# A Mamba-2 mixer block on one Trainium2 core: the decay matrices of two heads in one tile, with one exponential and one product for both

## The chip, the cores and the metric

The kernel runs on one core of one Trainium2 chip. The metric is the device time of one execution in microseconds (us), as the median of several runs. The engines have the names that the profile uses: PE (TensorE, matrix products), PEld (its loading of stationary operands), DVE (VectorE), ACT (ScalarE), POOL (GpSimd) and SP (SyncE, which issues the DMAs here). Each engine takes its instructions in order from a queue of its own, and engines wait for each other on semaphores.

## What is computed

One encoder block on a sequence of 1024 positions with 1024 channels in float32: a mixer (a gated convolution branch and a Mamba-2 branch, merged) and a gated feed-forward network, each with its normalisation. The change lies in the Mamba-2 branch. It has 32 heads of 64 channels in 4 groups of 8 heads; the heads of a group share the state inputs B and C of width 128. Cut to what matters here, the reference does in every chunk

```python
acs = jnp.cumsum(ak, axis=1)                      # ak = dt * a, per head
seg = acs[:, :, None] - acs[:, None, :]
decay = jnp.exp(jnp.where(causal, seg, -jnp.inf)) # one matrix per head
cb = jnp.einsum("blgn,bsgn->blsg", ck, bk)        # one matrix per group
y_diag = jnp.einsum("blsg,blsgj,bsgjp->blgjp", cb, decay, xk)
```

and adds the part that comes from the state of the chunks before, multiplies by a gate and normalises over a group. So each head needs the matrix `decay * cb`, and this product is what the change touches.

## The kernel before

The sequence is cut in two halves of 512 positions (`hf` 0 and 1), and the channels lie on the 128 partitions, so nearly every tile is 128 x 512. Every large matrix product is made of three float32r products (high part by high part, high by low, low by high), so PE has most of the work. The program has three parts: the first input projections (to about 650 us), the stage with the Mamba-2 branch and the remaining projections (about 650 to 1200 us, after which the feed-forward part follows).

In the middle stage two streams of work are woven into each other. The main stream is a list of projection steps (`p0_..`, `p1_..`, `co..`, `s0_..`, `wo..`), each 24 matmuls of 512 columns into a PSUM tile that DVE or ACT then empties; before its matmuls a weight block is split into a high part `wh` (ACT, L163) and a low part `wl` (DVE, L164). The PSUM tiles of these steps are a ring of three, so a step can start only when the step three before it has been emptied: in the groups of the SSM's inputs that is the last of the DVE steps of a short convolution, `xo` (L1109), after three steps `p` (L1106). The second stream is `ssd` (L495 and on), a generator that is advanced a little after every second matmul row, and beside it run the convolution branch and a few smaller ones. A scheduler then puts the instructions of all streams in an order for each engine, from its own model of the times; so an instruction that gets another shape can move others around it.

`ssd` handles one group of one half: 4 chunks of 128 positions, 4 pairs of heads (`j`). For each pair a `Decay` object makes the two matrices M:

- `load` (L550): two DMAs, each a broadcast of one head's row of cumulative sums over 128 partitions, into two tiles of 512 columns (4 chunks of 128). There are four such tiles, so two pairs can be under way.
- `exp(e)` for head e (L553 to L559): four ACT steps of 128 columns (a Relu of the difference; the bias is a column that differs by chunk), then one exponential over 512 columns.
- `mul(e)` (L562): one DVE product of 512 columns with `cbm`, the masked C B matrix of the group.

The matrices are then the moving operands of 16 small matmuls `yd` (L623; two heads by four chunks, two passes each), which also frees the tiles for the pair after the next. Beside them `yo` (L608) multiplies C by the state, E (L613) scales that, and L625 to L629 put the pair's output `y` together. The squares of the four y of a group are summed into `say` (L329), PE sums that over the partitions (`scy`, or `sc` further on, L264), and DVE makes a reciprocal square root `ry` from it in small steps (L275 to L283). PE transposes that (L292), it goes through memory, and it scales the four `y` (L652), which are written to memory and come back as operands `Hh`, `Hl` of the steps `s0_..` and `s1_..` (L217, L218). Names carry half and group: `yd033` belongs to half 0, group 3, pair 3.

The calls of the three steps of a `Decay` stand at fixed places in `ssd`: in the first four chunks for the first pair of a group, and after the output of pair j for pair j + 1.

Of the kernel before, what the change touches and what calls it, by code (L numbers as in the profile page):

```python
# [6 lines left out]
F32 = mybir.dt.float32  # L7
F32R = mybir.dt.float32r
I32 = mybir.dt.int32
AF = mybir.ActivationFunctionType  # L10
ALU = mybir.AluOpType
# [3 lines left out]
P = 128  # L15
T = 512
# [3 lines left out]
J = 8  # L20
# [50 lines left out]
def build(tc, ins, outs):  # L71
# [33 lines left out]
    act = nc.scalar.activation  # L105
    vec = nc.vector
# [388 lines left out]
    def ssd(hf, g, D):  # L495
        sp = pools["b"]
# [18 lines left out]
        for c in range(NCK):  # L515
# [3 lines left out]
        cbm = sp.tile([P, T], F32, tag="cbm", name=f"cbm{hf}{g}")  # L519
        vec.tensor_tensor(out=cbm.rearrange("p (c l) -> p c l", l=P), in0=pcb.rearrange("p (c l) -> p c l", l=P),  # L520
                          in1=tri.unsqueeze(1).to_broadcast([P, NCK, P]), op=ALU.mult)
# [19 lines left out]
            S.append(sn)  # L541

        class Decay:
            def __init__(self, j):
                self.heads, self.M = [g * J + 2 * j + e for e in range(2)], []

            def load(self):
                for hd in self.heads:
                    m = sp.tile([P, T], F32, tag="M", name=f"M{hf}{hd}", bufs=4)
                    dma(out=m, in_=acs_d[hf, hd:hd + 1, :].to_broadcast([P, T]))  # L550
                    self.M.append(m)

            def exp(self, e):  # L553
                hd, m = self.heads[e], self.M[e]
                for c in range(NCK):
                    sl = slice(c * P, (c + 1) * P)
                    act(out=m[:, sl], in_=m[:, sl], func=AF.Relu, scale=-1.0,  # L557
                        bias=acs[:, c * 32 + hd:c * 32 + hd + 1])
                act(out=m, in_=m, func=AF.Exp, scale=-1.0)  # L559

            def mul(self, e):
                vec.tensor_tensor(out=self.M[e], in0=self.M[e], in1=cbm, op=ALU.mult)  # L562

        last = hf == NH - 1
        M = Decay(0)
        sn = None
        for c in range(NCK):
            px = pstile(f"xT{hf}{g}{c}")
            for j in range(4):
                nc.tensor.transpose(out=px[:, j * P:(j + 1) * P], in_=xs[j][:, c * P:(c + 1) * P], identity=ident)  # L570
            xd = sp.tile([P, T], F32, tag="xdt", name=f"xdt{hf}{g}{c}", bufs=4)
            vec.tensor_tensor(out=v3(xd), in0=v3(px), in1=heads(dt, c, g), op=ALU.mult)
            xdt.append(xd)
            if c > 0:
                next_state(c - 1, sn)
            if not (last and c == NCK - 1):
                wx = sp.tile([P, T], F32, tag="wx", name=f"wx{hf}{g}{c}", bufs=2)
                for h in range(J):
                    hs = slice(h * 64, (h + 1) * 64)
                    o = c * 32 + g * J + h  # L580
                    act(out=wx[:, hs], in_=px[:, hs], func=AF.Copy, scale=wdec[:, o:o + 1])
                wxs.append(wx)
            if c == 0:
                M.load()
            elif c == 1:
                M.exp(0)
            elif c == 2:
                M.exp(1)
            else:
                M.mul(0)  # L590
                M.mul(1)
            yield 1
            if not (last and c == NCK - 1):
                sn = new_state(c)
            yield 1
# [3 lines left out]
        for j in range(4):  # L599
            E = sp.tile([P, T], F32, tag="E", name=f"E{hf}{g}{j}", bufs=2)  # L600
            for e in range(2):
                hd = g * J + 2 * j + e
# [12 lines left out]
            if j < 3:  # L615
                M = Decay(j + 1)
# [11 lines left out]
            vec.tensor_tensor(out=pdg[:, c0:], in0=E[:, c0:], in1=pdg[:, c0:], op=ALU.add)  # L628
            vec.tensor_tensor(out=y, in0=y, in1=pdg, op=ALU.mult)  # L629
            if j < 3:  # L630
                M.exp(0)
            yield 1
            if j < 3:
                M.exp(1)
            sq.add(y)
            ys.append(y)
            yield 1
            if j < 3:
                M.mul(0)
                M.mul(1)  # L640
        D["end", g] = (sq, ys)

    def ssd_norm(hf, g, D):
# [1130 lines left out]
```

## Time and profile before

| | us |
|---|---|
| median of 3 runs | 2087.94 |
| lowest and highest run | 2082.25, 2089.29 |
| the profiled execution, its own time | 2084.13 |
| its span, first to last instruction | 2082.4 |
| mean granted TensorE clock | 0.975 |

The profile is of one execution. Busy time counts the time in which an engine runs an instruction; a mean duration is that of one instruction from start to end, and two instructions on one engine can overlap, so the distance from one start to the next is shorter than the duration. In a row of the timeline the first number is the start in us from the start of the span, the second the length of the merged piece; a bracket at the end gives the idle time of the engine before it and what ended that. In the rows of groups the numbers behind the count are the busy time in us and the mean in ns. Tile names are given there without half and group (`M`, `xo`, `yd`).

### The profile page before, as it was taken

Reading aid. Unit: us, or ns where it says so; the run is one execution under the profiler, and the core shown is the slowest. Engines: PE = TensorE matmul, PEld = TensorE weight load, DVE = VectorE, ACT = ScalarE, POOL = GpSimd, SP = SyncE. Lnnn points to the kernel's source line nnn. Section 1 sums busy time; section 2 is a strip of 40 time slices with the busy share of each in tenths; the row PEclk is TensorE's granted clock in tenths of the full one; section 3 lists DMA queues with packets and bytes.
Section 4 is the critical chain, followed back from the end, with each engine's and each line's share of the span. In section 5 each row is a group of like instructions: output and inputs, shape, how many; then the busy total and the mean of one; then the engine's idle time right before and its main releaser. Section 6 shows DMA issues by size and latency. Waiting matters only on the chain.

```text
span 2082.4 us, 26179 instructions
## 1 busy us (share of the span) xinstructions
PE 1941.3 (93%) x8802; PEld 1548.7 (74%) x8802; DVE 1574.0 (76%) x2458; ACT 1004.0 (48%) x1938; POOL 646.8 (31%) x487
## 2 busy tenths in 40 slices
PE   4899899999998899998899999998999999989997
PEld 3788688887876677776677777776888888767876
DVE  8878989878797978989797965759543443699655
ACT  4644454443444867566555733335333333444243
POOL 0008688888870000100000000005443443331400
PEclk9999999999998999999999999999999999999998
DMA  9232222323326867789898777761422222577653
GB/s 348 86 105 93 76 97 102 116 86 107 104 86 215 271 198 237 243 294 304 266 315 264 239 247 245 250 241 64 154 81 86 85 73 101 186 244 234 202 174 119
DMA packets 163958, 366.43 MB, mean 176 GB/s; under 512 B 18744, under 2 KB 19184, under 8 KB 163824
## 3 DMA queue, kind: packets, MB, share of 16 engines
q1 hardware_dynamic: 163824, 364.77, 52.6%
q8 instruction: 69, 1.13, 0.2%
q14 instruction: 65, 0.53, 0.1%
HBM read 281.57 MB, written 83.13 MB: 175 GB/s over the span
## 4 chain that ended last, share of the span: by engine, by line
PE 59%; DVE 20%; DMA 12%; issue 4%; ACT 3%; POOL 1%; SPq 0%; DVEq 0%; ACTq 0%; POOLq 0%
PE uXp L817 10%; PE uXf L817 10%; PE uZp L817 5%; PE uZf L817 5%; PE uXd L817 3%; PE uYp L817 2%; PE uYf L817 2%; DMA M<-acs_d 2%; PE s L189 2%; PE s L187 2%; PE s L188 2%; DMA E<-eac_d 2%; DMA wa_f<-in 1%; DVE gc L1128 1%; DMA wa_m<-in 1%
## 5 line engine op out<-in xcount | busy, mean ns | idle before, releaser
L163 ACT ACTIVATE wh<-w 128x1024 fp32r<-128x1024 f32 (+1 forms) x110 | 113.4, 1032 | 108.6 <-PE s L188 37.4
L164 DVE TENSOR_TENSOR wl<-w,wh 128x1024 fp32r<-128x1024 f32 (+1 forms) x110 | 130.7, 1189 | 23.3 <-ACT wh L163 15.8
L531 POOL TENSOR_TENSOR S<-S,dt_etot 128x512 f32<-128x512 f32 x16 | 20.5, 1281 | 294.7 <-ACT S L538 138.5
L557 ACT ACTIVATE M<-M,dt_acs 128x128 f32<-128x128 f32 x256 | 80.0, 394 | 59.4 <-DMA M<-acs_d 58.6
L930 POOL TENSOR_TENSOR fw<-fw,fw 128x512 f32<-128x512 f32 x37 | 59.5, 1608 | 120.2 <-DMA fw<-in 118.6
L672 DVE SCALAR_TENSOR_TENSOR pcM<-u,cw_eo,pcM 128x512 f32<-128x512 f32 x120 | 90.2, 752 | 2.5
L672 DVE SCALAR_TENSOR_TENSOR pcQ<-u,pc,pcQ 128x512 f32<-128x512 f32 x112 | 84.3, 753 | 2.7
L187 PE MATMUL s<-Hh,wh 128*128 128x512 f32 x192 | 76.4, 402 | 6.3 <-ACT Hh L217 4.0
L672 DVE SCALAR_TENSOR_TENSOR pcR<-u,pc,pcR 128x512 f32<-128x512 f32 x104 | 78.4, 754 | 2.7
L189 PE MATMUL s<-Hh,wl 128*128 128x512 f32 x192 | 76.8, 400 | 3.6 <-DVE wl L164 3.6
L187 PE MATMUL p<-Hh,wh 128*128 128x512 f32 x144 | 62.3, 453 | 18.0 <-DVE xo L1109 9.0
L188 PE MATMUL s<-Hl,wh 128*128 128x512 f32 x192 | 77.1, 402 | 0.9 <-DVE Hl L218 0.8
L845 POOL TENSOR_TENSOR b<-Hh,Hl 128x512 f32<-128x512 f32 x4 | 5.9, 1480 | 223.3 <-DVE spare L329 211.9
L817 PE MATMUL uXp<-T2h,dp 128*128 128x512 f32 x216 | 72.0, 395 | 3.0 <-ACT dp L795 3.0
L817 PE MATMUL uZp<-B22h,ep 128*128 128x512 f32 x216 | 72.4, 397 | 2.2 <-POOL ep L796 1.6
L817 PE MATMUL uYp<-Hh,bp 128*128 128x512 f32 x216 | 72.8, 399 | 1.0 <-DVE s1g L997 1.0
L817 PE MATMUL uXp<-T3h,fp 128*128 128x512 f32 x216 | 72.0, 396 | 1.2 <-ACT s L985 0.9
L817 PE MATMUL uXp<-T4h,gp 128*128 128x512 f32 x216 | 72.5, 396 | 0.4 <-DVE s5c L997 0.4
L817 PE MATMUL uZp<-T1h,cp 128*128 128x512 f32 x216 | 72.0, 395 | 0.0
L817 PE MATMUL uXp<-Hh,ap 128*128 128x512 f32 x216 | 71.0, 390 | 0.0
L188 PE MATMUL p<-Hl,wh 128*128 128x512 f32 x144 | 61.3, 427 | 5.4 <-DVE Hl L346 5.4
L817 PE MATMUL uZf<-T1h,cf 128*128 128x512 f32 x176 | 59.4, 401 | 3.5 <-DVE g L997 3.5
(565 smaller groups left out, 6412.5 us busy)
## 6 DMA issues: line engine op xcount, KB each, us to landing
fw<-in SPq DMA_DIRECT2D x134, 512.0 KB, 3.3
w<-in SPq DMA_DIRECT2D x100, 512.0 KB, 5.1
M<-acs_d SPq DMA_DIRECT2D x64, 256.0 KB, 4.9
wa_f<-in SPq DMA_DIRECT2D x48, 256.0 KB, 3.7
wa_m<-in SPq DMA_DIRECT2D x16, 512.0 KB, 9.3
xs<-xbc_d SPq DMA_DIRECT2D x32, 256.0 KB, 6.0
E<-eac_d SPq DMA_DIRECT2D x64, 128.0 KB, 6.2
y<-z_d SPq DMA_DIRECT2D x32, 256.0 KB, 5.5
```

Source lines behind the costliest of these rows:

```text
L163: act(out=hi, in_=w[:, :nk * P], func=AF.Copy)
L164: eng.tensor_tensor(out=lo, in0=w[:, :nk * P], in1=hi.bitcast(F32), op=ALU.subtract)
L187: nc.tensor.matmul(out=out, lhsT=whi[:, sl], rhs=rh, start=first and i == 0, stop=False)
L188: nc.tensor.matmul(out=out, lhsT=whi[:, sl], rhs=rl, start=False, stop=False)
L189: nc.tensor.matmul(out=out, lhsT=wlo[:, sl], rhs=rh, start=False, stop=last and i == n - 1)
L531: gp.tensor_tensor(out=v3(sn), in0=v3(S[c]), in1=heads(etot, c, g), op=ALU.mult)
L557: act(out=m[:, sl], in_=m[:, sl], func=AF.Relu, scale=-1.0, bias=acs[:, c * 32 + hd:c * 32 + hd + 1])
L672: vec.scalar_tensor_tensor(out=pt if k < n - 1 else out or pt, in0=src(k), scalar=w(k), in1=pt, op0=ALU.mult, op1=ALU.add)
L817: nc.tensor.matmul(out=out, lhsT=l[:, sl], rhs=r, start=first and k == 0 and i == 0, stop=k == 3 and i == 2, skip_group_check=True)
L845: gp.tensor_tensor(out=t, in0=H[k][0].bitcast(F32), in1=H[k][1].bitcast(F32), op=ALU.add)
L930: e[8].tensor_tensor(out=a21, in0=a11, in1=a21, op=ALU.subtract)
L1128: vec.scalar_tensor_tensor(out=t[:, d:], in0=src[:, :T - d], scalar=wc(k), in1=t[:, d:], op0=ALU.mult, op1=ALU.add)
```

## The change

The two heads of a pair get one tile `both` of 128 x 1024, two of them in turn in place of four of 512, so the memory is the same. The two DMAs and the eight Relu steps stay, each on its half of the tile. The two exponentials become one over 1024 columns, behind the Relu steps of the second head; the two products become one over 1024 columns, whose second operand `cbm` is read twice. The matmuls take the two halves as they took the two tiles.

```diff
         class Decay:
             def __init__(self, j):
-                self.heads, self.M = [g * J + 2 * j + e for e in range(2)], []
+                self.heads = [g * J + 2 * j + e for e in range(2)]
+                self.both = sp.tile([P, 2 * T], F32, tag="M", name=f"M{hf}{g}{j}", bufs=2)
+                self.M = [self.both[:, e * T:(e + 1) * T] for e in range(2)]
             def load(self):
-                for hd in self.heads:
-                    m = sp.tile([P, T], F32, tag="M", name=f"M{hf}{hd}", bufs=4)
+                for hd, m in zip(self.heads, self.M):
                     dma(out=m, in_=acs_d[hf, hd:hd + 1, :].to_broadcast([P, T]))
-                    self.M.append(m)
-            def exp(self, e):
+            def relu(self, e):
...
-                act(out=m, in_=m, func=AF.Exp, scale=-1.0)
-            def mul(self, e):
-                vec.tensor_tensor(out=self.M[e], in0=self.M[e], in1=cbm, op=ALU.mult)
+                if e:
+                    act(out=self.both, in_=self.both, func=AF.Exp, scale=-1.0)
+            def mul(self):
+                m3 = self.both.rearrange("p (e t) -> p e t", t=T)
+                vec.tensor_tensor(out=m3, in0=m3, in1=cbm.unsqueeze(1).to_broadcast([P, 2, T]), op=ALU.mult)
...
-                M.exp(0)
+                M.relu(0)
...
-                M.exp(1)
+                M.relu(1)
...
-                M.mul(0)
-                M.mul(1)
+                M.mul()
```

The scheduler orders the middle stage anew: outside it the order of the two programs is the same on PE, DVE and ACT. Below are three places. A row is the line, the operation, what it writes and reads with a running number behind each name, and the shape. Before, the M tiles are named by half and head (`M02` and `M03` are heads 2 and 3 of half 0); in the change by half, group and pair (`M001` is heads 2 and 3 of group 0).

On DVE, in the first group of the stage, the rows behind the weight split `wl28`, before:

```order
L164 TENSOR_TENSOR wl28_5610<-w28_5513,wh28_5609 128x1024
L1106 SCALAR_TENSOR_TENSOR p0_14_5519<-pre0_6_5591,pc_94,p0_14_5519 128x512
L1109 SCALAR_TENSOR_TENSOR xo013_5496<-pre0_5_5497,p0_13_5428 128x512
L1106 SCALAR_TENSOR_TENSOR p0_14_5519<-pre0_6_5591,pc_94,p0_14_5519 128x512
L249 ISA wa_m8_00_6262,as_m8_0_6415<-wa_m8_00_6262,rw_96,pc_94 128x512
```

The same place in the change:

```order
L1108 SCALAR_TENSOR_TENSOR p0_14_5515<-pre0_6_5584,pc_94,p0_14_5515 128x512
L576 TENSOR_TENSOR xdt003_5377<-xT003_5372,dt_dt0_1796 128x512
L1108 SCALAR_TENSOR_TENSOR p0_14_5515<-pre0_6_5584,pc_94,p0_14_5515 128x512
L249 ISA wa_m8_00_6245,as_m8_0_6395<-wa_m8_00_6245,rw_96,pc_94 128x512
L249 ISA as_m8_0_6395 128x1
L329 TENSOR_TENSOR sav0_5142<-sav0_5142,sqv0_6_5554 128x512
L540 TENSOR_TENSOR S001_5319<-S001_5319,st001_5334 128x512
L723 TENSOR_TENSOR ud0_7_5558<-ud0_7_5558,bcmean0_5066 128x512
L566 TENSOR_TENSOR M001_5469<-M001_5469,cbm00_5190 128x1024
L1108 SCALAR_TENSOR_TENSOR p0_14_5515<-pre0_6_5584,pc_94,p0_14_5515 128x512
L1111 SCALAR_TENSOR_TENSOR xo013_5492<-pre0_5_5493,p0_13_5425 128x512
```

The step `xo013`, which empties a PSUM tile, has moved behind eight instructions that followed it before (the accumulator read, the second row of L249, isn't counted).

On DVE, about 90 rows further, the last addition into the sum of squares `say00` of that group, before:

```order
L164 TENSOR_TENSOR wl33_6048<-w33_5932,wh33_6047 128x1024
L562 TENSOR_TENSOR M08_5958<-M08_5958,cbm01_5910 128x512
L562 TENSOR_TENSOR M09_5960<-M09_5960,cbm01_5910 128x512
L1106 SCALAR_TENSOR_TENSOR p0_23_5938<-pre0_9_6031,pc_94,p0_23_5938 128x512
L562 TENSOR_TENSOR M010_6193<-M010_6193,cbm01_5910 128x512
L562 TENSOR_TENSOR M011_6195<-M011_6195,cbm01_5910 128x512
L329 TENSOR_TENSOR say00_5452<-say00_5452,sqy00_3_5835 128x512
```

and in the change:

```order
L566 TENSOR_TENSOR M010_5930<-M010_5930,cbm01_5898 128x1024
L566 TENSOR_TENSOR M011_6178<-M011_6178,cbm01_5898 128x1024
L281 SCALAR_TENSOR_TENSOR tv0_5739<-r_ln0_126 128x4
L1111 SCALAR_TENSOR_TENSOR xo021_5829<-pre0_22_5830,p0_21_5778 128x512
L329 TENSOR_TENSOR say00_5449<-say00_5449,sqy00_2_5730 128x512
L1108 SCALAR_TENSOR_TENSOR p0_22_5852<-pre0_8_5904,pc_94,p0_22_5852 128x512
L576 TENSOR_TENSOR xdt010_5936<-xT010_5931,dt_dt0_1796 128x512
L282 TENSOR_TENSOR tv0_5739<-tv0_5739,vv0_5738 128x4
L329 TENSOR_TENSOR say00_5449<-say00_5449,sqy00_3_5823 128x512
L1108 SCALAR_TENSOR_TENSOR p0_22_5852<-pre0_8_5904,pc_94,p0_22_5852 128x512
L164 TENSOR_TENSOR wl33_6034<-w33_5920,wh33_6033 128x1024
```

The last addition now stands ahead of `wl33`, and `xo021` stands behind the products of the next group's first two pairs.

On PE, the last pair of group 3 of half 0, `yd033`, before:

```order
L189 MATMUL p1_24_8364<-Oh7_5124,wl32_8293 128x512
L292 MATMUL sc_6239<-ident_92,ry02_7482 4x128
L623 MATMUL yd033_7949<-M030_7866,xdt030_7442 64x128
L623 MATMUL yd033_7949<-M031_7868,xdt030_7442 64x128
...
L187 MATMUL p1_25_8446<-Oh0_5110,wh33_8360 128x512
```

and in the change:

```order
L187 MATMUL s0_00_8458<-Hh7_117,wh72_8387 128x512
L626 MATMUL yd033_7901<-M033_7821,xdt030_7407 64x128 x2
L626 MATMUL yd033_7901<-M033_7821,xdt031_7463 64x128 x2
L626 MATMUL yd033_7901<-M033_7821,xdt032_7520 64x128 x2
L626 MATMUL yd033_7901<-M033_7821,xdt033_7584 64x128 x2
L188 MATMUL s0_00_8458<-Hl7_118,wh72_8387 128x512
```

The pair has moved behind the 24 matmuls of `p1_25` and 22 of the 24 of `s0_00`.

More of the change, by code (lines that the diff above doesn't have):

```diff
@@ L630, in ssd @@
             if j < 3:
-                M.exp(0)
+                M.relu(0)
             yield 1
             if j < 3:
-                M.exp(1)
+                M.relu(1)
             sq.add(y)
@@ L638, in ssd @@
             if j < 3:
-                M.mul(0)
-                M.mul(1)
+                M.mul()
         D["end", g] = (sq, ys)
```

## The prediction

> **What bounds the kernel now.** I read the page first, then the busy times by stretches of the middle stage, then what PE waited for there, then the rows of the M tiles, and last the timeline at the longest waits.
>
> ```profile
> span 2082.4 us, 26179 instructions
> ## 1 busy us (share of the span) xinstructions
> PE 1941.3 (93%) x8802; PEld 1548.7 (74%) x8802; DVE 1574.0 (76%) x2458; ACT 1004.0 (48%) x1938; POOL 646.8 (31%) x487
> ```
>
> PE is busy for 93% of the span. The change takes nothing from PE, so it can gain only where PE stands idle, and only in the middle stage. This is that stage, by stretches (columns: length, then busy us and instructions of PE, PEld, DVE, ACT and POOL, granted clock, DMA share, GB/s); the first two rows are its most crowded stretch and the one behind it, the last is the sum from 650 to 1200 us.
>
> ```profile
> 700.00:750.00 50.00, 41.45 (x210) 32.96 (x209) 49.65 (x93) 38.84 (x95) 1.94 (x8) 0.83 0.71 227
> 750.00:800.00 50.00, 49.61 (x269) 36.25 (x267) 35.78 (x62) 29.86 (x75) 2.08 (x2) 1.00 0.71 222
> ...
> sum 550.00, PE 499.37 PEld 387.68 DVE 474.26 ACT 357.50 POOL 31.35; mean PE 45.40 PEld 35.24 DVE 43.11 ACT 32.50 POOL 2.85
> ```
>
> PE is idle for 550 - 499.37 = 50.6 us of the stage; no gain can be larger than that. DVE is full from 700 to 750 us (49.65 of 50), and there PE loses 8.5 us. Over the stage DVE is busy for 86% and ACT for 65%. What ended PE's waits (us in total, times, longest):
>
> ```profile
> PE p L187 <- DVE xo L1109: 10.7, 4, 8.5
> PE yo L608 <- DVE E L613: 6.2, 2, 4.8
> ...
> PE yd L623 <- DVE M L562: 3.1, 2, 1.6
> PE yd L623 <- ACT M L557: 2.9, 1, 2.9
> ```
>
> The 8.5 us stand at the entry of the stage, ahead of the first M. M itself accounts for 3.1 + 2.9 = 6.0 us in three waits. So the matrices are seldom what PE waits for, and a cheaper M is mostly hidden behind the projections.
>
> **The instructions that become fewer.** There are 64 exponentials and 64 products (busy us, mean ns, then idle time ahead of them):
>
> ```profile
> L562 DVE TENSOR_TENSOR M<-M,cbm 128x512 f32<-128x512 f32 x64 | 42.4, 690 | 12.4 <-ACT M L559 12.3
> ...
> L559 ACT ACTIVATE M<-M 128x512 f32<-128x512 f32 x64 | 38.5, 623 | 0.1
> ```
>
> They become 32 each of 1024 columns. The trace has that width on both engines in the splitting of weights, on DVE also as a product of two tiles' form:
>
> ```profile
> L164 DVE TENSOR_TENSOR wl<-w,wh 128x1024 fp32r<-128x1024 f32 x94 | 115.5, 1229 | 15.1 <-ACT wh L163 13.0 <-issue 2.0
> ```
>
> ```profile
> L163 ACT ACTIVATE wh<-w 128x1024 fp32r<-128x1024 f32 x94 | 99.9, 1064 | 75.6 <-PE s L188 37.4 <-DMA w<-in 13.9 <-PE co L188 10.8
> ```
>
> By the means a pair would save 2 x 690 - 1229 = 151 ns on DVE and 2 x 623 - 1064 = 182 ns on ACT. But instructions of one engine overlap, so what counts is the distance from start to start. On DVE:
>
> ```profile
> 709.49 1.29 DVE L562 TENSOR_TENSOR M<-M,cbm 128x512 f32<-128x512 f32 x2
> 710.69 0.75 DVE L346 SCALAR_TENSOR_TENSOR Ol<-xh_x1m,mod_m,Oh 128x512 fp32r<-128x512 f32 x1
> 711.35 0.75 DVE L625 SCALAR_TENSOR_TENSOR yd<-xs,pc,yd 128x512 f32<-128x512 f32 x1
> 712.01 1.22 DVE L164 TENSOR_TENSOR wl<-w,wh 128x1024 fp32r<-128x1024 f32 x1
> 713.14 0.75 DVE L346 SCALAR_TENSOR_TENSOR Ol<-xh_x1m,mod_m,Oh 128x512 fp32r<-128x512 f32 x1
> ```
>
> Two products take 710.69 - 709.49 = 1.20 us of the queue, one of 1024 takes 713.14 - 712.01 = 1.13. That is 0.07 us a pair, 2.2 us over 32 pairs (bounds: 0, if the operand that is read twice costs what two products cost, and 4.8 by the means). [...] On ACT:
>
> ```profile
> 707.91 1.14 ACT L559 ACTIVATE M<-M 128x512 f32<-128x512 f32 x2
> 708.96 0.71 ACT L344 ACTIVATE Oh<-xh_x1m,mod_m 128x512 fp32r<-128x512 f32 x1
> 709.57 1.05 ACT L163 ACTIVATE wh<-w 128x1024 fp32r<-128x1024 f32 x1
> 710.52 0.70 ACT L344 ACTIVATE Oh<-xh_x1m,mod_m 128x512 fp32r<-128x512 f32 x1
> ```
>
> Two exponentials take 1.05 us, one of 1024 columns 0.95: 3.2 us over 32 pairs (5.8 by the means).
>
> ACT's 3.2 us I cost at nothing: it is idle for a third of the stage and PE hides it; if it lay on the path, all 3.2 would count. DVE's 2.2 us count only where DVE is full and PE waits for it. That is one stretch, from about 686 to 750 us, with 6 of the 32 pairs: 6 x 0.07 = 0.4 us. **Term: -0.4 us** (0 to -4.8).
>
> **What is added: waits.** A wait for a second or third semaphore is an instruction of its own. The rows of them at `yd` and at the product:
>
> ```profile
> L623 PEldq EVENT_SEMAPHORE  x13: 51/51/51, 710.2 to 1185.8; - x13
> ```
>
> ```profile
> L562 DVEq EVENT_SEMAPHORE  x2: 21/21/21, 672.1 to 1036.1; - x2
> ```
>
> In the changed program the product also waits for the two DMAs that filled the halves (long landed by then), and so do the first matmuls. Counted in the two programs, the waits beyond the first rise from 2 to 50 on DVE and from 13 to 34 at `yd`. That is 48 x 21 ns = 1.0 us on DVE, of which 6 pairs in 32, 0.2 us, lie in the full stretch, and 21 x 51 ns = 1.1 us in PE's queue of weight loads. That queue runs ahead of the matmuls, so the cost there lies between 0 and 1.1; I take 0.5. **Term: +0.7 us** (0 to 2.1).
>
> **What comes later: the pair as a whole.** From the end of the second head's Relu steps, an exponential and a product had to follow: 0.62 + 0.69 = 1.31 us. Now it is the long ones, 1.06 + 1.23 = 2.29 us: a pair is ready 0.98 us later. On ACT and DVE the next instructions of the projections queue behind the long ones by half a microsecond at most. PE sees it only where M is what it waits for, and M ended three waits. Two stand at one pair:
>
> ```profile
> 720.87 0.66 PE L623 MATMUL yd<-M,xdt 128*64 128x128 f32 x2 [2.94 <-ACT M L557]
> 723.17 1.97 PE L623 MATMUL yd<-M,xdt 128*64 128x128 f32 x14 [1.64 <-DVE M L562]
> ```
>
> That is `yd003`, whose two products stood 2.4 us apart on DVE with other work between them; joined, nothing stands between them. That pair doesn't get later, the other one does. **Term: +1.0 us** (0 to 2.9, for three waits).
>
> **What moves: the full DVE stretch.** `xo013` moves behind eight instructions. With 0.60 us for a two-tile product (half of the 1.20), 0.66 for a SCALAR_TENSOR_TENSOR (two of them from 710.69 to 712.01), 1.13 for 1024 columns and 1.17 for the reduction of L249, this is 4 x 0.60 + 2 x 0.66 + 1.13 + 1.17 = 6.0 us:
>
> ```profile
> 685.90 1.23 DVE L164 TENSOR_TENSOR wl<-w,wh 128x1024 fp32r<-128x1024 f32 x1 [1.42 <-ACT wh L163]
> ...
> 689.02 1.17 DVE L249 CUSTOM_DVE_ANT_0 wa_m<-wa_m,rw,pc 128x512 f32<-128x512 f32 x1
> ```
>
> Before, `p0_20` waited for it thus:
>
> ```profile
> 688.50 0.50 PE L187 MATMUL p<-Hh,wh 128*128 128x512 f32 x1 [0.54 <-DVE xo L1109]
> ```
>
> Now it waits until 688.5 + 6.0 = 694.5; some 2 us of that PE fills with state and `yo` matmuls that stand ahead of it now, so 3 to 4 us are lost at once. But DVE, back to back from there on, does the same work whatever its order, and PE catches up: what counts is the last place at which PE waits for it. Before, that was the sum of squares:
>
> ```profile
> 742.16 1.70 PE L264 MATMUL scy<-ones,say 128*128 128x1 f32 x8 [2.38 <-DVE say L329]
> ```
>
> ```profile
> 741.42 0.69 DVE L329 TENSOR_TENSOR say<-say,sqy 128x512 f32<-128x512 f32 x1
> ```
>
> Adding DVE's prices from `wl28` (start 685.90) up to both events, the last `say00` comes after 55.0 us before and 52.2 now, so its wait of 2.38 us would go. But `xo021`, for which `p0_24` ahead of it waits, comes after 46.3 before and 49.6 now; with the 1.1 us by which my sum runs short of the trace at `say00` (741.42 + 0.69 = 742.1 against 741.0), that is 685.9 + 49.6 + 1.1 = 736.6. Matmuls start 0.23 us apart,
>
> ```profile
> 689.30 0.39 PE L187 MATMUL p<-Hh,wh 128*128 128x512 f32 x1
> 689.53 0.40 PE L188 MATMUL p<-Hl,wh 128*128 128x512 f32 x1
> ```
>
> so the 24 of `p0_24` end 5.5 us later, at 742.1: the same time as before. One stall takes the place of another. **Term: 0** (-2.4 if `xo021` is in time, +3.3 if all its delay comes through).
>
> **What moves: the rest of the stage.** From group 1 on, the SSM's small matmuls stand later among PE's projections, `yd033` by about 11 us of matmuls, and the two programs meet again at the end of half 1. The waits that hang on this are the 4.8 us at `yo`
>
> ```profile
> 948.28 1.65 PE L608 MATMUL yo<-bc,S 128*128 128x128 f32 x6 [4.83 <-DVE E L613]
> ```
>
> and 3.5 us at the steps that need the normalised y:
>
> ```profile
> 1060.69 1.22 PE L187 MATMUL s<-Hh,wh 128*128 128x512 f32 x2 [3.53 <-ACT Hh L217]
> ```
>
> From `yd030` to `yo033` PE has 13.3 us of matmuls in place of 12.1, by the same 0.23 us; the 4.8 should shrink by that difference. **Term: -1.2 us** (-8.4 if both go; the other end is the slower rival).
>
> **The sum** is -0.4 + 0.7 + 1.0 + 0 - 1.2 = +0.1 us against the profiled execution's own 2084.13 us. That execution is 3.8 us below the median of the three runs, and one run lies at 2082.25, so the change is smaller than the scatter. Put on the median: 2087.94 + 0.1 = **2088.0 us**.
>
> **The rivals.** *No change that can be measured* (forecast): within 0.3%, 6.3 us, about what a measurement of this kernel can tell from none. For it: PE is the bound, and M ends 6.0 us of its waits. Chance 0.47.
>
> *Faster*: the new order suits the chip better. The small matmuls stand later, when their operands are there. If the waits of 2.38, 4.83 and 3.53 us go, this is -10.7 us, with the other terms (+1.3) -9.4: 2078.5 us. For it: `yd` has been moved away from places where PE waited. Against it: that a stall moved on instead in the one stretch that I followed. Chance 0.28.
>
> *Slower*: PE runs out of projections behind the SSM. In group 0 of half 1 the program had about 40 large matmuls between `yd103` and the sum over `say10`, 9 us; now there are about 17, 4 us, while DVE still has 5.9 us of work between the two by the prices above. Between that sum and the transposed `ry10`, 4 large matmuls and a few small ones are left, 3 us, against 4.3 us on DVE. So PE waits there for about 2 + 1.3 us where it didn't, and a like squeeze at groups 2 and 3 of half 0, where the distance shrinks by 17 and 9 us, can cost as much each: +3 to +10, taken as +8: 2096 us. It decides where DVE's part is longer than the matmuls left. And a wait costs twice: from 700 to 750 us, where PE idles, the granted clock is 0.83, against 1.00 from 750 to 800 us, where PE is full. [...] Chance 0.25.
>
> *That it doesn't do what it says* would be a 1024-column product at the price of two; this is the upper end of the first term, and changes nothing else.
>
> **The range**: the faster rival's 2078.5 less the 4.4 us that DVE could gain beyond the first term gives 2074; the slower one's upper end, +10, with the other terms' upper ends (+2.1 and +2.9, less their values) gives 2101. Chances: faster 0.28, same 0.47, slower 0.25.
>
> **What would show it.** Right: 32 products of about 1.23 us and 32 exponentials of about 1.05; PE's idle time in the stage again near 50 us; in the stretch from 686 to 750 a wait of over 2 us for `xo` ahead of `p0_20`, and none left at `scy`. Wrong: PE idle time in the stage that differs by over 6 us; M as what ends more than 9 us of PE's waits (then the pair's delay was undersized); or waits for `say` or `ry` in half 1.

## The result, and the profile after

The change takes 2100.61 us (median of 14 runs, 2095.0 to 2111.73); the kernel before took 2087.09 us beside it (14 runs, 2080.37 to 2091.41). The ratio is 1.0058, with a 95% interval of 1.0044 to 1.0072: slower by about 12 us. That lies inside the range of the prediction, but what it held likeliest, no change, did not come; its slower rival did. Ratios here and below are those of the fast runs, and can differ a little from the ratio of the medians.

The profiled execution took 2095.0 us, the shortest of the 14. The head of its page:

```profile
span 2093.3 us, 26091 instructions
## 1 busy us (share of the span) xinstructions
PE 1946.2 (93%) x8802; PEld 1550.9 (74%) x8802; DVE 1573.4 (75%) x2426; ACT 1000.7 (48%) x1906; POOL 645.5 (31%) x487
```

DVE and ACT have 32 instructions less each, and are busy for 0.6 and 3.3 us less than before. PE runs the same 8802 matmuls, but is busy for 4.9 us longer (1946.2 against 1941.3), and it is idle for 6.0 us longer (147.1 of the span against 141.1). Together that is the 10.9 us by which the span has grown: half of it is waiting, and half is slower running. The groups of the joined instructions (busy us, mean ns, then idle time ahead of them):

```profile
L566 DVE TENSOR_TENSOR M<-M,cbm 128x1024 f32<-128x1024 f32 x32 | 40.4, 1267 | 5.5 <-ACT M L562 3.6 <-DMA wa_m<-in 1.9
L562 ACT ACTIVATE M<-M 128x1024 f32<-128x1024 f32 x32 | 33.8, 1055 | 0.3
```

A joined product takes 1267 ns against 2 x 690 before, a joined exponential 1055 against 2 x 623. That `cbm` is read twice costs nothing that can be seen. The change does what it says.

The stage by stretches (columns as in the prediction):

```profile
700.00:750.00 50.00, 42.50 (x217) 34.56 (x216) 49.12 (x90) 40.74 (x94) 1.58 (x6) 0.93 0.67 215
750.00:800.00 50.00, 50.00 (x273) 36.98 (x272) 36.52 (x60) 32.15 (x77) 3.07 (x2) 1.00 0.77 250
...
sum 550.00, PE 491.19 PEld 381.51 DVE 463.08 ACT 346.36 POOL 29.49; mean PE 44.65 PEld 34.68 DVE 42.10 ACT 31.49 POOL 2.68
```

The crowded stretch from 700 to 750 us is, if anything, better: PE is busy for 42.50 us there (41.45 before). But from 650 to 1200 us PE is busy for 491.19 us in place of 499.37: 8.2 us of idle time have been added to the 50.6. What ended PE's waits in the same stretch:

```profile
PE p L187 <- DVE xo L1111: 16.4, 5, 8.6
PE st L536 <- ACT wx L585: 6.1, 3, 3.2
PE xT L574 <- DMA xs<-xbc_d: 4.6, 3, 2.3
PE co L187 <- ACT Hh L749: 4.5, 1, 4.5
PE bT L510 <- DVE vv L275: 3.4, 1, 3.4
PE s L188 <- DVE Hl L218: 3.3, 2, 2.4
PE yd L626 <- issue: 3.2, 3, 2.2
```

No row names M, but the last one is M's: in each of its three waits the product ends 0.10 us before the matmul starts (why the profile then says "issue" is told below). So M's waits have shrunk from 6.0 to 3.2 us, and the 6.2 us at `yo` to 0.6. In their place stand waits for PSUM tiles that are not yet emptied (`xo`, 16.4 us against 10.7) and for operands of the projections and of the other streams. The list is no longer that of one bottleneck but of many small ones.

Where does PE fall behind? I gave every matmul its full name by counting along the order of each program, and compared when each projection and each step of the SSM ended (us, change less before):

| | main stream | second stream |
|---|---|---|
| entry of the stage | `p0_14` -2.9 | `yd003` -3.4 |
| group 1, half 0 | `p1_05` -6.5 | `yd013` -1.6 |
| group 2, half 0 | `co0_2` -12.9 | `yd023` +11.5 |
| group 3, half 0 | `p1_25` -9.4, `s0_00` -0.6 | `yd033` +12.3 |
| half 1 | `s0_06` -5.0, `wo0_7` -1.5 | `yd103` +17.3, `yd123` +15.4 |
| end of half 1 | `co1_1` +9.5, `co1_4` +8.9, `s1_00` +12.4 | `yd133` +11.3 |

About 3 us of this are no doing of the change: its profiled execution came to the stage that much sooner, and outside the stage the two orders are the same. In it the projections run ahead by up to 10 us more, and the SSM falls behind by 14 to 20. While there are projections left, that doesn't show in the main stream. At `co1_0` PE meets the end of the streams that run beside them, and waits. In the change (start, length, and in the bracket the idle time ahead and what ended it):

```profile
1197.92 1.22 PE L187 MATMUL co<-Hh,wh 128*128 128x512 f32 x2 [4.47 <-ACT Hh L749]
1206.58 1.80 PE L626 MATMUL yd<-M,xdt 128*64 128x128 f32 x16 [1.93 <-DVE E L616]
1212.37 0.73 PE L187 MATMUL co<-Hh,wh 128*128 128x512 f32 x2 [2.00 <-ACT Hh L749]
```

The `Hh` of these rows is not the SSM's: L749 is ACT's last step in the convolution branch's normalisation (half 1), whose eight outputs are the operands of `co1`. They came so in the change (duration min/median/max, first and last start):

```profile
L749 ACT ACTIVATE Hh<-un x8: 612/627/657, 1164.2 to 1211.7; 128x512 fp32r<-128x512 f32 x8
```

and so before:

```profile
L747 ACT ACTIVATE Hh<-un x8: 615/616/685, 1152.1 to 1197.4; 128x512 fp32r<-128x512 f32 x8
```

The eighth starts 14.3 us later. Before, PE waits at `co1_0` too, for 4.47 us, and for `Hl`, the low part that DVE makes of the same output (the first row of the second list below). The waits are not all that is lost there. These are PE's rows behind the third wait of the change:

```profile
1218.84 0.63 PE L187 MATMUL co<-Hh,wh 128*128 128x512 f32 x1
1219.27 0.63 PE L188 MATMUL co<-Hl,wh 128*128 128x512 f32 x1
...
1220.51 0.39 PE L188 MATMUL co<-Hl,wh 128*128 128x512 f32 x1
1220.74 0.39 PE L189 MATMUL co<-Hh,wl 128*128 128x512 f32 x1
```

The same matmuls start 0.43 us apart and then 0.23: up to 1220.5 us PE runs at about half its pace. Before, there was one such spell at this place, behind one wait:

```profile
1203.34 0.80 PE L188 MATMUL co<-Hl,wh 128*128 128x512 f32 x1 [4.47 <-DVE Hl L733]
1203.93 0.63 PE L189 MATMUL co<-Hh,wl 128*128 128x512 f32 x1
...
1213.06 0.56 PE L189 MATMUL co<-Hh,wl 128*128 128x512 f32 x1
1213.46 0.39 PE L187 MATMUL co<-Hh,wh 128*128 128x512 f32 x1
```

It lasts from 1203.3 to 1213.4, 10.1 us. The granted clock is 0.50 there, and by it the change has three such spells here: to 1203.4 (from 1196.6, but the first matmul starts at 1197.9), from 1206.8 to 1210.2 and from 1213.6 to 1220.5. In them PE runs for 15.7 us. Between the second and the third the clock is back at 1.00 (columns as in the prediction):

```profile
1209.00:1210.00 1.00, 1.00 (x4) 0.57 (x2) 1.00 (x2) 0.00 (x0) 0.00 (x0) 0.50 0.69 246
...
1212.00:1213.00 1.00, 0.63 (x2) 0.30 (x2) 1.00 (x2) 1.00 (x3) 0.00 (x0) 1.00 0.01 2
...
1214.00:1215.00 1.00, 1.00 (x4) 0.35 (x2) 1.00 (x3) 1.00 (x2) 0.00 (x0) 0.50 0.42 80
```

Before, it is 9.9 us without the idle time; of 5.8 us more at that pace, 1 - 0.23 / 0.43 = 47% are lost: 2.7 us. From the end of `wo0_7` to that of `co1_4` PE needs 46.2 us before and 56.6 in the change. Of these 10.4 us, 2.7 are slower running, 2.0 are idle time (8.9 against 6.9), and the rest, some 5.5, is 50 matmuls more (32 `yd`, 16 `yo` and 2 `st`), which have been put off until here: the lead at `wo0_7` was borrowed. The clock is at 0.50 for 10.2 us before and for 6.8, 3.4 and 6.8 us in the change. What sets these lengths, and why the second spell begins behind a wait of 1.93 us, no run here was made to show.

The borrowed lead also hides where PE stood idle. These are the stretches from the end of `p0_14` to that of `wo0_7`, and from there to that of `co1_4`, before:

```profile
678.80:1181.70 502.90, 464.06 (x2440) 360.04 (x2441) 437.47 (x804) 327.60 (x813) 31.05 (x31) 0.96 0.81 263
1181.70:1227.90 46.20, 39.34 (x187) 31.01 (x186) 37.78 (x75) 23.92 (x44) 0.00 (x0) 0.89 0.78 248
```

and in the change:

```profile
675.90:1180.20 504.30, 458.53 (x2390) 355.76 (x2390) 427.76 (x752) 318.33 (x771) 28.35 (x31) 0.96 0.80 258
1180.20:1236.80 56.60, 47.75 (x237) 36.81 (x237) 47.63 (x96) 29.07 (x53) 0.84 (x1) 0.85 0.69 225
```

In the first stretch PE is idle for 38.8 us before and 45.8 in the change, 7.0 more; in the second for 2.0 more. So most of the added waiting lies ahead of the end of half 1, spread over the waits of the list above. The main stream doesn't show it there, because it shares PE with 50 matmuls of the SSM less (2390 against 2440 in that stretch); at the end, when these fall due, the delay comes out.

### The profile page after: what moved, and what is told of

It is laid out like the page before. It is cut to its first block, busy times and chain, and to the rows that moved or that the text cites. A ratio compares the mean times of both kernels' runs of the same rounds, so it can differ in the third digit from the quotient of the medians.

```text
span 2093.3 us, 26091 instructions
## 1 busy us (share of the span) xinstructions
PE 1946.2 (93%) x8802; PEld 1550.9 (74%) x8802; DVE 1573.4 (75%) x2426; ACT 1000.7 (48%) x1906; POOL 645.5 (31%) x487
## 4 chain that ended last, share of the span: by engine, by line
PE 54%; DVE 21%; DMA 14%; issue 4%; ACT 3%; POOL 1%; SPq 1%; DVEq 0%; ACTq 0%; POOLq 0%
PE uXf L819 10%; PE uXp L819 10%; PE uZp L819 5%; PE uZf L819 5%; PE uYf L819 2%; PE uYp L819 2%; DMA M<-acs_d 2%; PE uXd L819 2%; DMA w<-in 2%; PE s L187 1%; PE s L189 1%; PE s L188 1%; DVE gc L1130 1%; DVE wl L164 1%; DMA yl<-y_d 1%
## 5 line engine op out<-in xcount | busy, mean ns | idle before, releaser
L187 PE MATMUL p<-Oh,wh 128*128 128x512 f32 x144 | 58.9, 409 | 7.4 <-DVE xo L1111 7.4
## 6 DMA issues: line engine op xcount, KB each, us to landing
wa_m<-in SPq DMA_DIRECT2D x16, 512.0 KB, 10.2
```

Of the source, the lines that this page charges most:

```text
L187: nc.tensor.matmul(out=out, lhsT=whi[:, sl], rhs=rh, start=first and i == 0, stop=False)
```

## Experiments: one part at a time

Three theories stood at the start. *Order*: the scheduler gave another order, and PE waits because of it. *Latency*: the joined pair is ready later. *Tile*: a tile for two heads brings coarser waits. The first four kernels undo parts of the change, or alter the pace at which the SSM is woven in.

One tile, but instructions of 512 columns (`tile_only`):

```diff
-                if e:
-                    act(out=self.both, in_=self.both, func=AF.Exp, scale=-1.0)
+                act(out=m, in_=m, func=AF.Exp, scale=-1.0)
...
-                m3 = self.both.rearrange("p (e t) -> p e t", t=T)
-                vec.tensor_tensor(out=m3, in0=m3, in1=cbm.unsqueeze(1).to_broadcast([P, 2, T]), op=ALU.mult)
+                for m in self.M:
+                    vec.tensor_tensor(out=m, in0=m, in1=cbm, op=ALU.mult)
```

> One tile of 1024 columns per pair as in the change, but two exponentials and two products of 512 columns as before. Three theories are put to all runs of this call. ORDER: the 12 us come from the place that the order gives the SSM's small matmuls among the projections on PE; the joined instructions themselves cost under 2 us. LATENCY: a pair that is ready about 1 us later, in a ring of two pairs, slows the SSM's stream wherever the order puts it. TILE: the joined tile's coarser dependencies and added waits cost it. Counted in 512-column matmuls from p0_14 on, this order stands within 1 us of the old one up to bT02, is 7 us earlier at yd023 and 5 us at yd033, and up to 8 us later at yd123 (the change: 14 later, 11 later, 14 later). ORDER: 2083 to 2091 us, not told apart from before. LATENCY: 2087, since no pair is ready later. TILE: about 2099, as the change.

Measured: 2094.89 us, ratio 1.0044 (1.0026 to 1.0062).

The second part of that diff alone leaves the joined exponential (`exp_joined`), the first part alone the joined product (`mul_joined`).

> One tile per pair and one exponential of 1024 columns, but two products of 512. The order puts yd023 and yd033 10 us earlier than before, yd100 27 us earlier, yd123 3 us earlier. ORDER: no slower than before: 2080 to 2088 us. LATENCY: the pair is ready 0.43 us later (1.05 - 0.62), less than half of the change's 0.98: +4 to +6, 2091 to 2093 us. TILE: about 2099.

Measured: 2104.03 us, ratio 1.0071 (1.0045 to 1.0098).

> One tile per pair and one product of 1024 columns, but two exponentials of 512. The order puts yd022 21 us later than before (the change: 20), yd023 11 later (14), yd033 11 later (11), yd103 4 later (9), yd123 8 later (14). ORDER: slower, by half to all of the change's loss: 2093 to 2100 us. LATENCY: the pair is ready 0.5 us later: +5 to +6, 2092 to 2094 us. TILE: about 2099.

Measured: 2097.37 us, ratio 1.0050 (1.0031 to 1.0068).

The change at another pace (`joined_rate09`):

```diff
-SSD_RATE = 0.85
+SSD_RATE = 0.9
```

> The change with nothing altered but the pace at which the SSM's stream is drawn when the program is written: 0.90 in place of 0.85. Every joined instruction stays. The order now puts yd023 and yd033 5 us earlier than before (the change: 14 and 11 later), yd103 14 earlier, yd123 14 earlier and yd133 16 earlier. ORDER: the loss goes, 2083 to 2090 us. LATENCY and TILE: it stays, 2096 to 2102 us.

Measured: 2104.11 us, ratio 1.0079 (1.0057 to 1.0101).

All four are slower, by 0.4 to 0.8%, and `exp_joined` and `joined_rate09` by more than any of the three theories had put. My order theory, as I had put it, falls: it wanted the SSM's *lateness* to be what costs, and `exp_joined` and `joined_rate09`, which place the SSM earlier than before, are the slowest. The numbers speak for the tile, which all four have in common. But all four also have orders of their own, and `tile_only` showed that this had to be taken apart: by the same comparison of names it stays within 2.4 us of before up to `p1_15`, as long as the two orders agree, and is 6.9 us late at `co0_0`, behind the place where they part.

## Experiments: the order held

A scheduler's order can be pinned. Between two instructions of one queue one can declare an edge that says "issue after" and waits for nothing. So I took from each program the order of every engine and of the DMA queue, and chained the other program's instructions in it. Both programs write their instructions down in the same sequence but for the joined ones, so each instruction has its partner. Where one joined instruction stands for two, it takes the place of the second; where two stand for one, they follow each other directly.

```diff
+        for a, b in zip(seq, seq[1:]):
+            tc.add_manual_dep(mine[b], mine[a].name,
+                              mybir.DependencyInfo(mybir.DependencyClass.NoSync, mybir.DependencyReason.DATA),
+                              reason="order")
...
     with tile.TileContext(nc, schedule_with_timeline_sim=True) as tc:
         build(tc, ins, outs)
+        _hold(tc, ORDERS)
```

Here `mine` are the instructions of one engine as the program writes them and `seq` the order to hold. The change, in the order of before (`joined_old_order`):

> The change with its joined tile, exponential and product, but with every engine and the DMA queue held in the order of the program before: the joined instruction stands where the second of its two stood, all else is where it was. After the first four runs (tile 2094.9, exponential alone 2104.0, product alone 2097.4, other pace 2104.1) the theory that only a late SSM costs time is out. Left are: ANY ORDER, the old order suits the chip better than the others that come out of the scheduler, whichever way they differ, and the joined instructions cost under 2 us; and OPERATIONS, the joined tile with its waits, and the pair that is ready later, cost 7 to 17 us themselves. ANY ORDER: 2085 to 2090 us, not told apart from before. OPERATIONS: 2095 to 2104 us.

Measured: 2089.25 us, ratio 1.0002 (0.9986 to 1.0018).

The kernel before, in the order of the change (`split_new_order`):

> The kernel before with its four tiles of 512 columns, two exponentials and two products per pair, but with every engine and the DMA queue held in the order of the change; the two small instructions stand directly behind each other where the joined one stands. ANY ORDER: 2098 to 2103 us, as the change. OPERATIONS: 2085 to 2090 us.

Measured: 2103.14 us, ratio 1.0054 (1.0036 to 1.0072).

One tile with split instructions, in the order of before (`tile_old_order`; the diff of `tile_only` and the one above):

> One tile for two heads with two exponentials and two products of 512, held in the order of the program before on every engine. The first run of this form, in an order of its own, took 2094.9 us. ANY ORDER: 2085 to 2090 us. OPERATIONS (the tile's coarser waits): 2093 to 2097 us.

Measured: 2087.88 us, ratio 0.9988 (0.9974 to 1.0003).

That settles it. The joined operations in the old order cost nothing that can be measured; the old operations in the new order lose 0.54% of the change's 0.58%. And the tile, which in its own order lost 0.44%, loses nothing in the old one, so the theory of the tile falls. The page of `split_new_order` has all the old instructions, and PE waits at the same places as in the change:

```profile
span 2097.7 us, 26165 instructions
...
PE 1947.4 (93%) x8802; PEld 1550.1 (74%) x8802; DVE 1577.5 (75%) x2458; ACT 1002.4 (48%) x1938; POOL 645.4 (31%) x487
```

```profile
PE co L187 <- ACT Hh L747: 6.8, 3, 4.0
PE st L536 <- ACT wx L581: 6.3, 3, 3.3
...
PE bT L510 <- DVE vv L275: 3.5, 1, 3.5
```

`joined_old_order` also shows what the joined pair costs by itself, since nothing else has moved. The M chain at `yd003`:

```profile
720.90 1.23 DVE L566 TENSOR_TENSOR M<-M,cbm 128x1024 f32<-128x1024 f32 x1
721.32 1.04 ACT L562 ACTIVATE M<-M 128x1024 f32<-128x1024 f32 x1
722.20 1.60 PEld L626 LDWEIGHTS yd<-M,xdt 128*64 128x64 f32 x16 [5.38 <-issue]
722.23 1.98 PE L626 MATMUL yd<-M,xdt 128*64 128x128 f32 x16 [5.22 <-issue]
```

The product ends at 720.90 + 1.23 = 722.13, the matmul starts at 722.23: it waited for M, though the profile says "issue" (a wait for several semaphores, the last of which it cannot name). The same holds for all five waits entered so at `yd`, where the product ends 0.09 to 0.10 us ahead of the matmul. So this row of its list of waits is M's:

```profile
PE yd L626 <- issue: 11.8, 5, 5.2
```

11.8 us in five waits, against 3.1 + 2.9 in three before. The latency theory has its mechanism right: the pair is later, and PE waits 5.8 us longer for it. But the span is 2083.4 against 2082.4 us, and the interval of the ratio ends at +3.8 us: not all of that waiting becomes time. By the comparison of names `wo0_7` ends 5.0 us later than before and `s1_00`, behind the stage, 2.9 us later. Where the 2.1 us between the two come back I did not follow; the last 1.9 come back where the two programs are the same, so they are a difference between executions.

Does a new order cost as much where no operation is altered at all? The kernel before, with another pace (`before_rate095`):

```diff
-SSD_RATE = 0.85
+SSD_RATE = 0.95
```

> The kernel before with nothing altered but the pace at which the SSM's stream is drawn when the program is written: 0.95 in place of 0.85. No instruction differs in shape; the scheduler gives another order (yd023 and yd033 5 us of matmuls earlier, yd123 5 us earlier, bT02 24 us earlier). ANY ORDER: slower like the others, 2094 to 2104 us. OPERATIONS: no penalty, 2083 to 2091 us.

Measured: 2123.79 us, ratio 1.0159 (1.0138 to 1.0180): far slower than the change itself, and outside both ranges.

## Experiments: where in the order

Three kernels with the change's operations hold one order up to a step and the other behind it, on all engines; they differ only in the table of the order. A fourth, `joined_old_pe`, holds PE's queue alone; it is shown against `joined_old_order` (`pe_old` and the like stand for the encoded lists of places).

```diff
-ORDERS = {"PE": pe_old, "Activation": act_old, "DVE": dve_old, "Pool": pool_old, "SP": sp_old}
+ORDERS = {"PE": pe_old}
```

> The change with all its joined instructions and with PE's order alone held as in the program before; ACT, DVE and the DMA queue are ordered anew by the scheduler around it (about 700 instructions stand elsewhere than before, by some 4 places). That the order is the cause is settled by now: joined in the old order 1.0002, split in the new order 1.0054. This run asks whose order. PE'S QUEUE (the place of the SSM's matmuls among the projections): 2085 to 2091 us. THE VECTOR ENGINES' QUEUES (what stands ahead of the SSM's and the convolution's steps there): 2094 to 2102 us.

Measured: 2112.98 us, ratio 1.0106 (1.0086 to 1.0127). Neither answer was right. PE in the old order with the other queues in a new one is worse than either order as a whole. So it isn't PE's order that was the good one, but that of all queues together: as I read it, what counts is whether DVE, ACT and the DMA queue deliver in the order in which PE asks.

The new order up to `p1_05`, behind it the old one (`new_until_p1_05`):

> The change, held in its own order on all engines up to the projection p1_05, and from there in the order of the program before. In the trace of the change p1_05 ended 6.5 us sooner than before and yd013 1.6 sooner. If that lead is a gain, the old order keeps some of it: 2081 to 2087 us, better than both. If the lead is only borrowed from the SSM's stream, which is put off, it is paid back by the end of the half: 2087 to 2091. If the loss comes from this entry part (the 6 us by which p0_20 waits longer): 2094 to 2100.

Measured: 2090.57 us, ratio 1.0002 (0.9990 to 1.0013). The entry of the stage, with the move of `xo013`, is harmless; the lead it gives isn't kept.

The new order up to `s0_00`, behind it the old one (`new_until_s0_00`):

> The change, held in its own order up to s0_00, which lies behind the SSM of half 0, and from there in the old order. There the projections of the change stand level with before (s0_00 0.6 us sooner), but yd033 came 12.3 us later. LAG (the SSM's delay at the end of half 0 is carried to the end of half 1 and costs PE there): the loss stays, 2095 to 2101 us. SECOND HALF (the loss is made by the order of half 1 itself, behind s0_00): 2086 to 2091 us.

Measured: 2093.53 us, ratio 1.0015 (0.9999 to 1.0030).

The old order up to `s0_00`, behind it the new one (`old_until_s0_00`):

> The counterpart: the change held in the old order up to s0_00, then in its own. LAG: 2086 to 2092 us, since there is no delay to carry. SECOND HALF: 2096 to 2102 us. If both this run and its counterpart are slow by half, the loss is shared.

Measured: 2105.71 us, ratio 1.0071 (1.0054 to 1.0087).

Most of the loss is made behind `s0_00`, by the order of half 1. The order up to there accounts for 0.15%, and that can only just not be told from nothing. The SSM's delay in half 0 is not needed: in `old_until_s0_00` there is none (`yd033` is 0.9 us sooner than before), and of the three it is the slowest. The two losses don't add up to exactly that of the change (0.86 against 0.58%); the order behind `s0_00` was made for another state of the streams. From 965 to 1250 us, in one row each (columns as above), before:

```profile
965.00:1250.00 285.00, 260.24 (x1368) 203.88 (x1367) 236.04 (x434) 162.66 (x382) 13.31 (x11) 0.96 0.83 271
```

the change:

```profile
965.00:1250.00 285.00, 254.81 (x1332) 197.15 (x1330) 227.94 (x404) 155.01 (x361) 12.55 (x11) 0.95 0.82 260
```

`joined_old_order`:

```profile
965.00:1250.00 285.00, 259.23 (x1354) 204.41 (x1353) 237.01 (x421) 161.31 (x367) 12.79 (x11) 0.94 0.83 270
```

and `old_until_s0_00`:

```profile
965.00:1250.00 285.00, 248.96 (x1294) 192.33 (x1294) 227.78 (x407) 154.78 (x361) 12.95 (x11) 0.94 0.81 255
```

PE is busy for 260, 255, 259 and 249 of the same 285 us. DVE and ACT get through less too in the change and in `old_until_s0_00`, and neither is full: the engines wait for each other. And `old_until_s0_00` waits for `Hh` at `co1` as the change does, only longer (9.6 us in three waits, of which the two long ones are shown, against 6.5 in two):

```profile
1204.68 1.22 PE L187 MATMUL co<-Hh,wh 128*128 128x512 f32 x2 [4.98 <-ACT Hh L749]
...
1213.98 1.09 PE L626 MATMUL yd<-M,xdt 128*64 128x128 f32 x16 [2.20 <-DVE E L616]
...
1220.48 1.22 PE L187 MATMUL co<-Hh,wh 128*128 128x512 f32 x2 [4.11 <-ACT Hh L749]
```

Over all fourteen kernels, the start of the last `Hh` of the convolution branch (half 1) goes with the end of `co1_1` on PE (us, each from its own trace):

| kernel | last `Hh` starts | `co1_1` ends | ratio |
|---|---|---|---|
| before | 1197.4 | 1205.4 | 1 |
| `tile_old_order` | 1200.4 | 1207.5 | 0.9988 |
| `joined_old_order` | 1201.7 | 1209.1 | 1.0002 |
| `new_until_p1_05` | 1202.8 | 1208.5 | 1.0002 |
| `new_until_s0_00` | 1207.7 | 1214.8 | 1.0015 |
| `tile_only` | 1211.4 | 1215.5 | 1.0044 |
| the change | 1211.7 | 1214.9 | 1.0058 |
| `split_new_order` | 1212.4 | 1215.9 | 1.0054 |
| `mul_joined` | 1214.8 | 1218.7 | 1.0050 |
| `old_until_s0_00` | 1219.8 | 1223.4 | 1.0071 |
| `joined_rate09` | 1219.8 | 1222.5 | 1.0079 |
| `exp_joined` | 1223.2 | 1229.8 | 1.0071 |
| `joined_old_pe` | 1228.5 | 1237.6 | 1.0106 |
| `before_rate095` | 1240.6 | 1244.7 | 1.0159 |

That the two go together doesn't say which drives which: the convolution's steps wait in the queues of DVE and ACT behind others that wait for PE (in the change, near 1129 us, 1.43 us at `wh` on ACT and 0.80 us at `E` on DVE). In `exp_joined`, `joined_rate09` and `joined_old_pe` the main stream is 28 to 35 us late already at `wo0_7`, ahead of any wait for this `Hh`; there the late `Hh` is part of a delay that came about earlier. In the change and in `old_until_s0_00` PE is seen to wait for this `Hh`. Other orders lose in other ways: `joined_rate09` waits 21.4 us at `yd` (five waits, entered as "issue") and not for `Hh` at `co1`; `before_rate095` loses 26 us between `wo0_7` and `co1_0`, in waits for M, `Hl` and `Hh` by turns. What in the order of half 1 makes this `Hh` late was not tried; it would take a kernel that moves the convolution's steps alone.

No version is shown to be faster than the kernel before. `tile_old_order` comes nearest, and its interval takes in 1.

## Why the prediction came out as it did

1. **Fewer instructions** (forecast -0.4 us): right as far as can be seen. The joined instructions have the predicted lengths, and DVE's and ACT's savings stay hidden; 0.4 us is less than these runs can tell.
2. **Added waits** (+0.7): not measured by themselves, but with the terms 1 and 3 they cost next to nothing. The wait instructions at the product and in PE's queue of weight loads in the trace of the change:

```profile
L566 DVEq EVENT_SEMAPHORE  x29: 21/50/520, 669.4 to 1201.1; - x29
L626 PEldq EVENT_SEMAPHORE  x21: 51/51/6359, 697.2 to 1203.6; - x21
```

   They are fewer than I had counted from the programs (29 and 21 rows, not 50 and 34), and their shortest still takes 21 and 51 ns.
3. **The pair as a whole** (+1.0, 0 to 2.9): the wait was undersized, 5.8 us at `yd` in `joined_old_order`; the cost cannot be told from the forecast. Together the first three terms were +1.3; held in the old order, the change costs 0.4 us by the ratio (-2.9 to +3.8), 1.0 by the span.
4. **The full DVE stretch** (0): right, by `new_until_p1_05`, where only this part of the order is new (1.0002). Of the two signs, the wait at `scy` is gone as forecast; the wait ahead of `p0_20` came under another name. In the change at that place:

```profile
676.38 0.50 PE L187 MATMUL p<-Hh,wh 128*128 128x512 f32 x1 [0.45 <-ACT wh L163]
687.94 2.07 PE L536 MATMUL st<-wx,btok 128*128 128x512 f32 x2 [3.20 <-ACT wx L585]
...
740.27 0.94 PE L264 MATMUL scy<-ones,say 128*128 128x1 f32 x8
```

   PE stands idle for 3.20 us where I had put 3 to 4, before the state matmul `st`, which the new order has put ahead of `p0_20`; `p0_20` itself starts at 691.66, just as `xo013` ends (691.61). The stall that was to take the place of the one at `scy`, at `p0_24` behind `xo021`, is only 0.42 us; longer ones came at `yd` (2.19) and `bT` (3.44) instead. So the sum of this stretch is right, and its second stall is not.
5. **The rest of the stage** (-1.2 us): this step failed. It measured about +11 (`split_new_order`: 0.54%). I looked at the waits that could *go*, and two of three went: the 4.83 and 2.38 us are no longer in the list, the 3.53 has become 2.57. I then took the list of the other waits as fixed. But with an order that is new over 550 us, every wait is drawn anew, and 8 us more came than went (58.8 against 50.6 us idle, past the 6 us that the prediction had named as a sign of being wrong). I had the SSM's small matmuls "later by about 11 us" and asked only what that saves; I didn't ask what the ring of PSUM tiles (`xo`) and the streams beside it, the convolution's normalisation among them, do when they come later too.

Of the rivals, *slower* came nearest: +8 forecast, 12 measured. Its kind is right in part: PE does run out of projections behind a stream that is late, but most of the idle time was added before that. Its places were wrong. It put the waits at `say10` and `ry10` in group 0 of half 1; there the change waits for neither (in all of half 1, 0.8 us for `ry`, in groups 1 and 3). The delay came out at the end of half 1, and the longest wait there was for the convolution's `Hh`. So that its price is near is luck, and so is that the measured time lies inside the range, 0.4 us below its upper end: that end was summed from waits that did not come. The sum is uneven, too: the faster rival's has the other terms' +1.3 in it, the slower one's has not; with them its 2096 would be 2097. That a wait costs twice, for which its sum holds nothing, agrees with the totals: beside 6.0 us more of idle time PE was busy for 4.9 us longer with the same matmuls. *Faster* had named the waits that do go, and did not reckon with new ones.

The chances carried a hint that I didn't use. The sum said "no change" because the terms that I could price cancelled; the term that I could not price was the whole order of the stage. Its range belonged in the forecast, and the runs show that more of it lies on the slow side: of the ten other orders that were timed (that of the change, those of the first four experiments, of `before_rate095`, and of the four of the last section) none is faster than the old one; two cannot be told from it, and eight lose 0.4 to 1.6%. Why the old order should be the best is not shown. Constants such as `SSD_RATE` may have been chosen for it; then any other would be likely to lose.

## What to carry to other kernels

Where a scheduler sets the order, a change of an instruction's shape is two changes: the instruction, and an order drawn anew over the whole stage; hold the order on all queues to measure the first alone, and the instruction in both forms to measure the second. Here ten other orders gave none that was faster and eight that were slower, by more than such an instruction can save off the critical path; so a kernel like this one is better compared with the old order kept and the new instruction in it. When waits that end at one operand vanish, ask which waits come in their place; and when one stream runs ahead, count what the others still owe before calling it a lead.

## What the runs showed of the hardware

- In the kernel before, behind a wait of 4.47 us that ended at 1203.3, PE ran for 10 us with 0.43 us from matmul to matmul in place of 0.23, at a granted clock of 0.50. In the change the clock was at 0.50 in three spells between 1196 and 1221 us, of 6.8, 3.4 and 6.8 us, the second of which began behind 1.93 us of idle time.
- A product of 1024 columns whose second operand is read twice takes 1267 ns (1239 in the old order), a plain two-operand instruction of that width 1229: the repeated operand costs 10 to 38 ns, if anything.
- A matmul that waits for M behind several semaphores is entered as "issue", although the product ends 0.09 to 0.10 us ahead of it (eight waits, in the change and in `joined_old_order`). Where a wait has no releaser in the list, the ends of the operands' last writers, in the timeline, name it.
- 5.8 us more of waits at one operand made the end of the stage (`s1_00`) 2.9 us later and the span 1.0 us longer (`joined_old_order`): the sum of PE's waits for an operand is not what it costs.
